# A group's scores and weights traced ahead of the previous group's outputs in the mLSTM heads of a hybrid diffusion step

## The chip, the cores and the metric

The kernel runs on one core of one Trainium2 chip. The metric is device time in microseconds (us) of one execution. The engines are called as the profile calls them: PE (TensorE: matmuls and transposes), DVE (VectorE), ACT (ScalarE), POOL (GpSimd), and SP, which issues most of the DMAs.

## The reference, cut to what matters

One layer of a backbone is applied to 1024 latent tokens and 256 context tokens, 1280 tokens in all, 1024 wide. The layer has three branches: centred pooling, spatial gating, and a bidirectional mLSTM with 4 heads of 128. The change lies in the mLSTM branch, which for a chunk of tokens computes

```python
m_t = jnp.maximum(inter, jnp.max(dmat, axis=2))
w_intra = jnp.exp(dmat - m_t[:, :, None, :])
w_inter = jnp.exp(inter - m_t)
s = jnp.einsum('bthd,bshd->btsh', qc, kc) * w_intra
num = jnp.einsum('btsh,bshd->bthd', s, vc) + w_inter[..., None] * jnp.einsum('bthd,bhde->bthe', qc, C)
den = jnp.sum(s, axis=2) + w_inter * jnp.einsum('bthd,bhd->bth', qc, n)
h = num / jnp.maximum(jnp.abs(den), jnp.exp(-m_t))[..., None]
```

once forward and once backward; the two `h` are added, normalised over each head and later gated. The other branches, the output projection and a feed-forward part follow.

## The kernel before, in words

Tokens are handled in ten chunks of 128, which form three groups (`GROUPS`): chunks 0 to 3, 4 to 7, and the context chunks 8 and 9. Dense projections use weights split in a high and a low part, three matmuls per product (`dense`, L117). `u`, the layer's normalised input, fills 40 of the 59 row buffers of the pool `sp` (`slot`, 128x512 each). A head's k, q and v fill 8 of them (`evict_kqv`, L343), `vn`, the rows of the gating branch, ten (L684).

`head` (L574) works on one head in this order.

- L575 to L591: transposes of k and v (tiles `tk`, `tv`), copied into parts of `z`, the row buffer of 128 x 10240 words that earlier held the input rows.
- L601 to L612: the scan over the chunks' states, matmuls `kv` and a DVE update each (L606), which leaves all states `S` in `z`.
- L615 to L667, a loop over the three groups, in two steps that the change pulls apart. The first (L619 to L641) makes scores and weights: scores `st` on PE (L622), row maxima spread over partitions `rb` (L626), then for each direction `w` = exp(rb + column terms + mask) times scores (L630, L632, L633) and `e` = exp(rb + state maximum) times q (L638, L640). The second (L642 to L667) makes the outputs: for each chunk `pv`, the product of `w` with v plus that of `e` with the state (L649, L651), the denominators (L654 to L656), both directions' sum in `hn` (L657, L658), squares (L659); then for the group the reciprocal root of the mean square (L129 on DVE, L130 on POOL), the scaling (L663), the transposes `th` (L664), the eviction `yc` (L666) and its DMA (L667).

The PSUM tiles `st`, `rb`, `pv`, `th`, `tk`, `tv`, `kv` share five buffers (`ps_sd`, L78); the dense products and `sv` share three others (`ps_mm`, L75). `w`, `e`, `yc` share five SBUF buffers (`tmp`, L72).

What is traced behind a head: the projections of the next one (`head_proj`, L565, L674), and behind the last head the gating branch's `sv` (L679 to L694): two column halves q of ten row tiles, 24 matmuls of 256 columns each, evicted by ACT into `vn[i]` (L693), for which half 0 takes row buffers. Its weights come in two parts per half; the low part is made by POOL (L94 with `eng=G`). Then come the pooling projections `xp` (L842 on) and the windows, which use `z` again.

The order on the engines is not that of the text. The framework plans it (`schedule_with_timeline_sim=True`, L1545): on each engine an instruction earlier in the text goes first among those that the plan holds to be ready, and later text fills what is left. From L276 to L431 the order is pinned by hand (`Pinned`, L35); the heads are not.

Of the kernel before, what the change touches and what calls it, by code (L numbers as in the profile page):

```python
# [14 lines left out]
P = 128  # L15
# [5 lines left out]
GROUPS = ((0, 512), (512, 512), (1024, 256))  # L21
# [27 lines left out]
def hybrid_step(  # L49
# [13 lines left out]
    pa, pw = ExitStack(), ExitStack()  # L63
# [5 lines left out]
    def slot(name, dt=F32R):  # L69
        return sp.tile([P, 512], dt, tag="s", name=name)  # L70

    def tmp(name, dt=F32):  # L72
        return tp.tile([P, 512], dt, tag="t", name=name)
# [4 lines left out]
    def ps_sd(name):  # L78
        return pp.tile([P, 512], F32, tag="sd", name=name, bufs=5)

    def small(shape, name, bufs=4):
        return cp.tile(shape, F32, tag=f"sm{shape[-1]}", name=name, bufs=bufs)
# [44 lines left out]
    def rstd_of(ssq, n, name):  # L127
        r = small([P, 16], f"rs_{name}")
        V.tensor_scalar(r[:, :n], ssq, 1.0 / n_of[name[0]], EPS, ALU.mult, ALU.add)  # L129
        G.tensor_tensor(r[:, :n], r[:, :n], neghalf[:, :n], ALU.pow)  # L130
        return r
# [8 lines left out]
    z = cp.tile([P, 10 * D], F32, name="z")  # L140
# [255 lines left out]
    for at, (g, k) in enumerate(steps):  # L396
# [3 lines left out]
        if (g, k) == (1, 2):  # L400
# [4 lines left out]
            for i in range(2):  # L405
                w = slot(f"wgs{i}").rearrange("p (k c) -> p k c", c=P)
# [28 lines left out]
    def chunks(ap):  # L435
        return ap.rearrange("p (c t) -> p c t", t=P)
# [80 lines left out]
    for g in range(3):  # L517
        t0, n = GROUPS[g]
# [34 lines left out]
    vaug = z[:, 1280:2570].rearrange("p (c t) -> p c t", t=129)  # L553
    vs = z[:, 2570:5150].rearrange("p (c d t) -> p c d t", d=2, t=129)
    S = z[:, 5150:7730].rearrange("p (c d t) -> p c d t", d=2, t=129)
    hn2 = [z[:, 9010 + i * 512 : 9522 + i * 512].rearrange("p (c t) -> p c t", t=P) for i in range(2)]

    def proj(idx, name, evict, eng=V, w=None, groups=range(3)):
# [6 lines left out]
    def head_proj(h):  # L565
        tiles = {}
        kq = kq0 if h == 0 else slot(f"kq{h}", F32)
        for nm, idx in (("k", I_K), ("v", I_V), ("q", I_Q)):
            w, lst = begun.pop(f"{nm}{h}", (None, []))
            tiles[nm] = lst  # L570
            proj(idx + h, f"{nm}{h}", lambda g, ps: lst.append(evict_kqv(nm, h, g, ps, kq)), w=w, groups=range(len(lst), 3))
        return tiles["k"], tiles["v"], tiles["q"]

    def head(h, kT, vT, qT):  # L574
        for g in range(3):  # L575
            t0, n = GROUPS[g]
            c0, ncn = t0 // P, n // P
            ps = ps_sd(f"tk{h}_{g}")
            for c in range(ncn):
                PE.transpose(ps[:, c * P : (c + 1) * P], kT[g][:, c * P : (c + 1) * P], ident)  # L580
            A.copy(knat[:, c0 : c0 + ncn, :], chunks(ps[:, :n]))
            ps = ps_sd(f"tv{h}_{g}")
            for c in range(ncn):
                PE.transpose(ps[:, c * P : (c + 1) * P], vT[g][:, c * P : (c + 1) * P], ident)
            A.copy(vaug[:, c0 : c0 + ncn, 0:P], chunks(ps[:, :n]))  # L585
            for d in range(2):
                e = EWS[:, c0 : c0 + ncn, d * 4 + h].unsqueeze(2).to_broadcast([P, ncn, P])
                V.tensor_tensor(vs[:, c0 : c0 + ncn, d, 0:P], chunks(ps[:, :n]), e, ALU.mult)  # L588
        V.memset(vaug[:, :, P : P + 1], 1.0)
        for d in range(2):  # L590
            V.tensor_copy(vs[:, :, d, P : P + 1], EWS[:, :, d * 4 + h : d * 4 + h + 1])  # L591

        def kv(c, d):
            ps = ps_sd(f"kv{h}_{c}_{d}")
            PE.matmul(ps[:, 0:129], knat[:, c, :], vs[:, c, d, :], start=True, stop=True)  # L595
            return ps[:, 0:129]

        def dc(c, d):
            return decb[:, d * 4 + h, c : c + 1]

        SP.dma_start(S[:, 0, 0, :], state[h, :, 0, :])  # L601
        SP.dma_start(S[:, 7, 1, :], state[h, :, 1, :])
        for i in range(7):
            for d in range(2):
                c, nx = (i, i + 1) if d == 0 else (7 - i, 6 - i)
                V.scalar_tensor_tensor(S[:, nx, d, :], S[:, c, d, :], dc(c, d), kv(c, d), ALU.mult, ALU.add)  # L606
        fin = tmp(f"fin{h}")[:, 0:258].rearrange("p (d t) -> p d t", d=2)
        for d in range(2):
            c, nx = (8, 9) if d == 0 else (9, 8)
            A.copy(S[:, nx, d, :], kv(c, d))  # L610
            V.scalar_tensor_tensor(fin[:, d, :], S[:, nx, d, :], dc(nx, d), kv(nx, d), ALU.mult, ALU.add)
        A.dma_start(st_out[h], fin)  # L612

        ssq = small([P, 16], f"ssq{h}")
        for g in range(3):  # L615
            t0, n = GROUPS[g]
            c0, ncn = t0 // P, n // P
            hn = hn2[(3 * h + g) % 2]
            st = ps_sd(f"st{h}_{g}")  # L619
            for c in range(ncn):  # L620
                s = slice(c * P, (c + 1) * P)
                PE.matmul(st[:, s], kT[g][:, s], qT[g][:, s], start=True, stop=True)  # L622
            pw, qw = [], []
            for d in range(2):
                rb = ps_sd(f"rb{h}_{g}_{d}")
                PE.matmul(rb[:, :n], selr[:, d * 4 + h : d * 4 + h + 1].to_broadcast([100, P]), rhl[g][0:100, :n], start=True, stop=True)  # L626
                w = tmp(f"w{h}_{g}_{d}")
                for c in range(ncn):
                    s = slice(c * P, (c + 1) * P)
                    V.scalar_tensor_tensor(  # L630
                        w[:, s], rb[:, s], GC[:, c0 + c, d * 4 + h : d * 4 + h + 1], masks[d], ALU.add, ALU.add)
                A.activation(w[:, :n], w[:, :n], AF.Exp)  # L632
                V.tensor_tensor(w[:, :n], w[:, :n], st[:, :n], ALU.mult)  # L633
                pw.append(w)
                e = tmp(f"e{h}_{g}_{d}")
                for c in range(ncn):
                    s = slice(c * P, (c + 1) * P)
                    A.activation(  # L638
                        e[:, s], rb[:, s], AF.Exp, bias=mpb[:, d * 4 + h, c0 + c : c0 + c + 1], scale=1.0)
                V.tensor_tensor(e[:, :n], e[:, :n], qT[g][:, :n], ALU.mult)  # L640
                qw.append(e)  # L641
            for cl in range(ncn):  # L642
                c = c0 + cl
                s = slice(cl * P, (cl + 1) * P)
                pv = ps_sd(f"pv{h}_{c}")
                pvv = pv[:, 0:258].rearrange("p (d t) -> p d t", t=129)
                for d in range(2):
                    inter = not (c == 8 and d == 0) and not (c == 9 and d == 1)
                    PE.matmul(pvv[:, d, :], pw[d][:, s], vaug[:, c, :], start=True, stop=not inter)  # L649
                    if inter:  # L650
                        PE.matmul(pvv[:, d, :], qw[d][:, s], S[:, c, d, :], start=False, stop=True)  # L651
                den = small([P, 2, 1], f"den{h}_{c}")
                em = EM[:, c, :].rearrange("p (d h) -> p d h", d=2)[:, :, h]
                A.activation(den[:, :, 0], pvv[:, :, P], AF.Abs)  # L654
                V.tensor_tensor(den[:, :, 0], den[:, :, 0], em, ALU.max)  # L655
                V.reciprocal(den, den)  # L656
                A.activation(hn[:, cl, :], pvv[:, 0, 0:P], AF.Copy, scale=den[:, 0, :])  # L657
                V.scalar_tensor_tensor(hn[:, cl, :], pvv[:, 1, 0:P], den[:, 1, :], hn[:, cl, :], ALU.mult, ALU.add)  # L658
                A.activation(vs[:, c, 0, 0:P], hn[:, cl, :], AF.Square, accum_out=ssq[:, c : c + 1])  # L659
            r = rstd_of(ssq[:, c0 : c0 + ncn], ncn, f"h{h}_{g}")  # L660
            ps = ps_sd(f"th{h}_{g}")
            for cl in range(ncn):
                A.activation(hn[:, cl, :], hn[:, cl, :], AF.Copy, scale=r[:, cl : cl + 1])  # L663
                PE.transpose(ps[:, cl * P : (cl + 1) * P], hn[:, cl, :], ident)  # L664
            yc = tmp(f"yc{h}_{g}")
            A.activation(yc[:, :n], ps[:, :n], AF.Copy, scale=ccol[:, C_GM + h : C_GM + h + 1])  # L666
            SP.dma_start(scr_yc[h, :, t0 : t0 + n], yc[:, :n])  # L667

    qkv = head_proj(0)
    for h in range(H):  # L670
        cur = qkv
        head(h, *cur)
        if h + 1 < H:
            qkv = head_proj(h + 1)  # L674
# [4 lines left out]
    for q in range(2):  # L679
        wq = [load_w(w_sv[q, hf], f"sv{q}_{hf}", eng=G) for hf in range(2)]  # L680
        for i in range(NT):
            g, o = (i * P) // 512, (i * P) % 512
# [356 lines left out]
    for ri, r in enumerate(ORDER):  # L1039
        scr = (scr_ya, scr_yb, scr_yc)[r]  # L1040
        ys = [[] for _ in range(4)]
        for g in range(3):
            for kc in range(4):
                t0, n = GROUPS[g]
# [10 lines left out]
        for d in range(KT):  # L1055
            if d % 2 == 0:
                wb = [load_half(w_branch[r, d // 2][:, i * 512 : i * 512 + 512], f"wb{r}_{d}_{i}") for i in range(2)]
            for g in range(3):
                t0, n = GROUPS[g]
# [494 lines left out]
```

## Time and profile before

| | us |
|---|---|
| three timed runs | 1955.17, 1954.14, 1947.21 |
| their median | 1954.14 |
| the profiled execution's own time | 1949.2 |
| its span, first to last instruction | 1947.4 |
| PE busy | 1910.0 |
| DVE busy | 1301.5 |
| ACT busy | 848.8 |
| POOL busy | 380.8 |
| the four heads, first `tk` to last `th` | 141.5 to 417.1 |

The timed runs lie within 8 us of each other. The profiled execution lies between the lowest of them and the median, 4.9 us below the median. "Busy" is the time in which an engine had at least one instruction of its kind under way; the granted clock beside it says how fast PE ran in that time. A wait is idle time of an engine, put down to the instruction that released it.

### The profile page before, as it was taken

Reading aid. Unit: us, or ns where it says so; the run is one execution under the profiler, and the core shown is the slowest. Engines: PE = TensorE matmul, PEld = TensorE weight load, DVE = VectorE, ACT = ScalarE, POOL = GpSimd, SP = SyncE. Lnnn points to the kernel's source line nnn. Section 1 sums busy time; section 2 is a strip of 40 time slices with the busy share of each in tenths; the row PEclk is TensorE's granted clock in tenths of the full one; section 3 lists DMA queues with packets and bytes.
Section 4 is the critical chain, followed back from the end, with each engine's and each line's share of the span. In section 5 each row is a group of like instructions: output and inputs, shape, how many; then the busy total and the mean of one; then the engine's idle time right before and its main releaser. Section 6 shows DMA issues by size and latency. Waiting matters only on the chain.

```text
span 1947.4 us, 28196 instructions
## 1 busy us (share of the span) xinstructions
PE 1910.0 (98%) x10142; PEld 1632.4 (84%) x10142; DVE 1301.5 (67%) x2234; ACT 848.8 (44%) x1771; POOL 380.8 (20%) x381
## 2 busy tenths in 40 slices
PE   9999998999999999999999999999999999999998
PEld 5878887988888888888888888888888888888886
DVE  6574345469597878776675589887766655654665
ACT  6443365542433333342113375555455545443443
POOL 1100011064022422220000015444431210000003
PEclk9999998999999999999999999999999999999999
DMA  9120111115443444459522435776774596655544
GB/s 371 74 73 33 42 42 39 34 57 186 139 165 129 157 141 153 146 198 363 187 93 98 152 119 213 252 270 243 260 260 140 188 333 202 207 176 151 161 137 161
DMA packets 152774, 318.56 MB, mean 164 GB/s; under 512 B 17934, under 2 KB 42226, under 8 KB 150586
## 3 DMA queue, kind: packets, MB, share of 16 engines
q1 hardware_dynamic: 109082, 223.35, 34.7%
q0 software_dynamic: 15520, 57.75, 7.9%
q10 hardware_dynamic: 28032, 35.67, 5.1%
q8 instruction: 79, 1.29, 0.3%
q14 instruction: 61, 0.50, 0.1%
HBM read 220.21 MB, written 95.98 MB: 162 GB/s over the span
## 4 chain that ended last, share of the span: by engine, by line
PE 65%; DMA 8%; POOL 4%; DVE 4%; issue 2%; ACT 1%; SPq 0%; POOLq 0%; ACTq 0%; DVEq 0%
PE w L1421 6%; PE w L1422 6%; PE w L1423 6%; DMA z<-in_w_ff 4%; POOL z L1260 3%; PE pb L1068 3%; PE pb L1069 3%; PE pb L1070 3%; DMA scr_t<-z 3%; PE fT_g L904 2%; PE fT_g L902 2%; PE fT_g L903 2%; PE po L1188 2%; PE po L1186 2%; PE po L1187 2%; PE fB_g L902 2%
## 5 line engine op out<-in xcount | busy, mean ns | idle before, releaser
L1260 POOL TENSOR_TENSOR z<-z 128x512 f32<-128x512 f32 x64 | 99.9, 1561 | 121.6 <-DMA z<-in_w_ff 118.9
L547 POOL PARTITION_ALL_REDUCE acc<-acc x16 | 54.4, 3437 | 224.5 <-DVE acc L541 148.1
L959 DVE TENSOR_TENSOR z<-z 128x512 f32<-128x512 f32 x120 | 95.3, 794 | 2.7
L541 DVE SCALAR_TENSOR_TENSOR acc<-z,scond,acc 128x512 f32<-128x512 f32 x112 | 82.2, 780 | 0.0
L1375 POOL TENSOR_TENSOR rs_y<-rs_y,neghalf 128x1 f32<-128x1 f32 x10 | 9.9, 989 | 332.5 <-DVE rs_y L1374 332.4
L1226 ACT ACTIVATE z<-z 128x512 f32<-128x512 f32 x64 | 40.5, 632 | 71.4 <-DVE z L968 38.8
L985 ACT ACTIVATE z<-z 128x512 f32<-128x512 f32 x56 | 35.3, 632 | 64.0 <-DVE z L968 18.6
L630 DVE SCALAR_TENSOR_TENSOR w<-rb,gcol,cst 128x128 f32<-128x128 f32 x80 | 21.8, 344 | 35.5 <-PE rb L626 35.5
L1074 DVE TENSOR_TENSOR sg<-pb,sg 128x512 f32<-128x512 f32 (+1 forms) x48 | 28.7, 600 | 24.3 <-PE pb L1070 24.2
L130 POOL TENSOR_TENSOR rs_h<-rs_h,neghalf 128x4 f32<-128x4 f32 (+1 forms) x12 | 11.8, 983 | 150.8 <-DVE rs_h L129 150.5
L1227 ACT ACTIVATE z<-z 128x512 f32<-128x512 f32 x64 | 40.3, 629 | 1.1
L750 POOL TENSOR_TENSOR z<-z 128x256 f32<-128x256 f32 (+13 forms) x20 | 37.6, 1888 | 12.7 <-ACT z L735 6.2
L893 ACT CAST hi_wb<-raw_wb 128x512 fp32r<-128x512 f32 x24 | 14.8, 620 | 56.4 <-PE pb L1069 45.7
L1189 DVE TENSOR_TENSOR po<-po,gt 128x512 f32<-128x512 f32 (+1 forms) x24 | 14.6, 607 | 35.5 <-PE po L1188 35.4
L1251 POOL DMA_DIRECT2D scr_s<-x x48 | 26.2, 547 | 54.8 <-DVE x L1245 49.1
L548 POOL TENSOR_TENSOR acc<-acc,bt 1x512 f32<-1x512 f32 x16 | 22.8, 1440 | 61.0 <-issue 61.0
L1192 ACT ACTIVATE po<-z 128x512 f32<-128x512 f32 (+1 forms) x24 | 12.7, 530 | 48.4 <-DVE z L1191 34.1
L606 DVE SCALAR_TENSOR_TENSOR z<-z,dmb,kv 128x129 f32<-128x129 f32 x56 | 17.0, 346 | 23.1 <-PE kv L595 23.0
L1075 DVE TENSOR_TENSOR z<-z,sg 128x512 f32<-128x512 f32 (+1 forms) x48 | 28.6, 600 | 1.1
L649 PE MATMUL pv<-z,w 128*128 128x129 f32 x160 | 25.9, 283 | 3.3 <-DVE w L633 3.3
L655 DVE TENSOR_TENSOR den<-den,gcol 128x2 f32<-128x2 f32 x40 | 6.8, 178 | 29.9 <-ACT den L654 29.2
L588 DVE TENSOR_TENSOR z<-tv,gcol 128x512 f32<-128x512 f32 (+1 forms) x24 | 14.4, 602 | 18.2 <-ACT z L585 17.9
(5350 smaller groups left out, 7248.7 us busy)
## 6 DMA issues: line engine op xcount, KB each, us to landing
z<-in_w_ff SPq DMA_DIRECT2D x64, 512.0 KB, 5.8
z<-in_w_ada SPq DMA_DIRECT2D x64, 256.0 KB, 3.1
scr_t<-z POOLq DMA_DIRECT2D x16, 1024.0 KB, 4.5
z<-in_w_in SPq DMA_DIRECT2D x28, 512.0 KB, 4.4
scr_g<-z ACTq DMA_DIRECT2D x48, 256.0 KB, 2.0
sg<-scr_g SPq DMA_DIRECT2D x48, 256.0 KB, 4.6
scr_h<-z ACTq DMA_DIRECT2D x48, 256.0 KB, 3.7
scr_s<-x POOLq DMA_DIRECT2D x48, 256.0 KB, 4.7
```

Of the source, the lines that this page charges most:

```text
L541: V.scalar_tensor_tensor(acc[j], raw, scond[:, k, j : j + 1], acc[j], ALU.mult, ALU.add)
L547: G.partition_all_reduce(acc[j], acc[j], P, bass.bass_isa.ReduceOp.add)
L902: PE.matmul(ps, whi[:, s], ahi, start=first and k == ks[0], stop=False)
L959: V.tensor_tensor(out, x, y, op)
L1068: PE.matmul(pb[:, :n], whi[:, s], yh, start=kc == 0, stop=False)
L1069: PE.matmul(pb[:, :n], whi[:, s], yl, start=False, stop=False)
L1070: PE.matmul(pb[:, :n], wlo[:, s], yh, start=False, stop=kc == 3)
L1226: A.activation(t, t, AF.Relu)
L1260: G.tensor_tensor(out, x, y, ALU.subtract)
L1421: PE.matmul(banks[j], h_[:, s], rh, start=fp == 0, stop=False)
L1422: PE.matmul(banks[j], l_[:, s], rh, start=False, stop=False)
L1423: PE.matmul(banks[j], h_[:, s], rl, start=False, stop=fp == NFP - 1)
```

## The change

The first step of a group becomes a function `weighted(g)` that returns the `w` and `e` tiles, the second a function `outputs(g, pw, qw)`. They are called in the order weighted(0), weighted(1), outputs(0), weighted(2), outputs(1), outputs(2). No instruction is added or removed, and no shape changes. Two groups' weights are alive at a time, so some of them move out of the five `tmp` buffers: the `w` tiles of group 1 go to two new views of `z` (columns 7730 to 8753), and the `e` tile of the backward direction of each group goes to the columns of `z` that the same group's `hn` takes afterwards. That leaves three `tmp` buffers for groups 0 and 2, one for group 1, and one for each `yc`.

```diff
+    wz = [z[:, 7730 + i * 512 : 8242 + i * 512] for i in range(2)]
+    hnz = [z[:, 9010 + i * 512 : 9522 + i * 512] for i in range(2)]
     hn2 = [z[:, 9010 + i * 512 : 9522 + i * 512].rearrange("p (c t) -> p c t", t=P) for i in range(2)]
...
         ssq = small([P, 16], f"ssq{h}")
-        for g in range(3):
+
+        def weighted(g):
             t0, n = GROUPS[g]
             c0, ncn = t0 // P, n // P
-            hn = hn2[(3 * h + g) % 2]
             st = ps_sd(f"st{h}_{g}")
...
-                w = tmp(f"w{h}_{g}_{d}")
+                w = wz[d] if g == 1 else tmp(f"w{h}_{g}_{d}")
...
-                e = tmp(f"e{h}_{g}_{d}")
+                e = hnz[(3 * h + g) % 2] if d == 1 else tmp(f"e{h}_{g}")
...
                 qw.append(e)
+            return pw, qw
+
+        def outputs(g, pw, qw):
+            t0, n = GROUPS[g]
+            c0, ncn = t0 // P, n // P
+            hn = hn2[(3 * h + g) % 2]
             for cl in range(ncn):
...
             SP.dma_start(scr_yc[h, :, t0 : t0 + n], yc[:, :n])
+
+        ahead = weighted(0)
+        for g in range(3):
+            following = weighted(1) if g == 0 else weighted(2) if g == 1 else None
+            outputs(g, *ahead)
+            ahead = following
```

## The prediction

> **What bounds the kernel now.** I read the page first, then the busy time by stretch over the heads, then PE's waits there, then the timelines around those waits.
>
> ```profile
> span 1947.4 us, 28196 instructions
> PE 1910.0 (98%) x10142; PEld 1632.4 (84%) x10142; DVE 1301.5 (67%) x2234; ACT 848.8 (44%) x1771; POOL 380.8 (20%) x381
> ...
> PEclk9999998999999999999999999999999999999999
> ```
>
> PE works for 1910.0 of 1947.4 us, so an edit that adds and removes no matmul can win at most the 37.4 us in which PE stands still, and what a lowered clock costs. The clock row has one slice below 9, the seventh (292 to 341 us), which lies in the third head. The page cannot say whose idle time the 37.4 us is, so I cut the heads at the first transpose `th` of each group.
>
> In the next rows the columns are the stretch, its length, then busy time and instructions of PE, PEld, DVE, ACT and POOL, the granted clock, the DMA share and GB/s.
>
> ```profile
> 164.00:184.80 20.80, 20.80 (x125) 18.40 (x124) 8.66 (x28) 9.93 (x35) 1.04 (x1) 1.00 0.12 36
> ...
> 261.80:276.40 14.60, 14.24 (x120) 13.80 (x119) 7.54 (x25) 10.11 (x35) 3.37 (x2) 1.00 0.18 60
> 276.40:284.70 8.30, 6.14 (x49) 5.51 (x47) 3.94 (x15) 4.92 (x19) 0.69 (x1) 1.00 0.08 32
> 284.70:300.20 15.50, 15.32 (x130) 15.08 (x131) 8.23 (x23) 5.55 (x19) 0.00 (x0) 1.00 0.03 10
> 300.20:313.10 12.90, 11.14 (x93) 10.51 (x92) 7.55 (x28) 8.33 (x35) 1.01 (x1) 1.00 0.06 17
> 313.10:329.20 16.10, 11.56 (x94) 10.98 (x94) 9.51 (x26) 11.29 (x40) 4.26 (x2) 0.95 0.13 46
> 329.20:339.90 10.70, 9.01 (x47) 8.44 (x47) 3.94 (x15) 6.02 (x23) 0.70 (x1) 0.60 0.23 86
> ...
> 357.40:375.70 18.30, 18.30 (x156) 18.21 (x155) 7.36 (x26) 11.08 (x46) 1.36 (x3) 1.00 0.02 9
> ```
>
> Length less PE's busy time, from 261.8 to 339.9: 0.36 + 2.16 + 0.18 + 1.76 + 4.54 + 1.69 = 10.7 us. That is the end of the second head and the whole third. In the first head (164 to 184.8) and the fourth (357.4 to 375.7) PE is never idle, though the same chain of steps runs there: later text fills it. So PE bounds the heads except where filler is short.
>
> What the 10.7 us wait for:
>
> ```profile
> PE th L664 <- ACT z L663: 6.3, 3, 4.5
> ...
> PE pv L649 <- DVE w L633: 3.3, 2, 1.6
> ```
>
> Before `th`, the transposes of the scaled outputs, 6.3 us in three waits; before `pv`, for the weights of the same group, 3.3 us in two. The remaining 1.1 us are small.
>
> And the clock:
>
> ```profile
> 328.00:332.00 4.00, 2.40 (x10) 2.00 (x10) 1.13 (x4) 1.60 (x5) 0.75 (x1) 0.50 0.71 254
> 332.00:336.00 4.00, 2.74 (x13) 2.77 (x14) 1.60 (x4) 2.76 (x10) 0.00 (x0) 0.50 0.17 66
> 336.00:340.00 4.00, 3.98 (x26) 3.78 (x26) 1.21 (x7) 2.17 (x11) 0.70 (x1) 0.77 0.00 0
> ```
>
> At clock 0.50 half of PE's busy time is lost: 2.40/2 + 2.74/2 + 3.98 x 0.23 = 1.2 + 1.4 + 0.9 = 3.5 us. It follows the longest wait. So the heads hold 10.7 + 3.5 = 14.2 us that a better order could win. The other 26.7 us of idle time lie outside 261.8 to 339.9 and have nothing to do with the loop.
>
> **Why filler is short, and what the change does to it.** The third head in PE's order:
>
> ```profile
> 307.77 1.06 PE L651 MATMUL pv<-z,e 128*128 128x129 f32 x8
> ...
> 313.07 0.33 PE L664 MATMUL th<-cst,z 128*128 128x128 f32 x1 [1.37 <-ACT z L663]
> 313.24 1.06 PE L622 MATMUL st<-qT,kT 128*128 128x128 f32 x8
> ...
> 318.11 0.83 PE L649 MATMUL pv<-z,w 128*128 128x129 f32 x6
> ...
> 324.43 0.28 PE L692 MATMUL sv<-lo_sv,u7c 128*128 128x256 f32 x1
> 329.24 0.47 PE L664 MATMUL th<-cst,z 128*128 128x128 f32 x1 [4.53 <-ACT z L663]
> ...
> 333.26 1.20 PE L649 MATMUL pv<-z,w 128*128 128x129 f32 x4 [1.63 <-DVE w L633]
> ...
> 335.83 0.56 PE L690 MATMUL sv<-hi_sv,u0h 128*128 128x256 f32 x1
> ```
>
> Two things are to be seen. First, `st` of the next group follows the first `th` of the group ahead at once (313.07, 313.24), and it does so in all eight places of the trace, though k and q have long been there. These are the first and the last:
>
> ```profile
> 174.71 0.39 PE L651 MATMUL pv<-z,e 128*128 128x129 f32 x2
> ...
> 184.78 0.49 PE L664 MATMUL th<-cst,z 128*128 128x128 f32 x3
> 185.10 0.39 PE L622 MATMUL st<-qT,kT 128*128 128x128 f32 x2
> ...
> 398.88 0.27 PE L664 MATMUL th<-cst,z 128*128 128x128 f32 x1
> 398.99 0.39 PE L622 MATMUL st<-kq 128*128 128x128 f32 x2
> ```
>
> The five PSUM buffers that `th` and `st` share seem to be handed out in the order of the text. So the plan cannot pull scores forward by itself; the text must. (The first head has 9.7 us of other work between the end of `pv` and `th`; the third has 4.3.) Second, no `sv` matmul runs between 324.43 and 335.83. The reason is in ACT's evictions of `sv`:
>
> ```profile
> 301.30 0.37 ACT L693 COPY vn<-sv 128x256 f32<-128x256 f32 x1 [0.85 <-PE st L622]
> ...
> 306.66 0.37 ACT L693 COPY vn<-sv 128x256 f32<-128x256 f32 x1 [0.76 <-DVE e L640]
> ...
> 314.33 0.37 ACT L693 COPY vn<-sv 128x256 f32<-128x256 f32 x1 [0.44 <-PE st L622]
> ...
> 319.70 0.37 ACT L693 COPY vn<-sv 128x256 f32<-128x256 f32 x1 [0.76 <-DVE e L640]
> ...
> 334.49 0.37 ACT L693 COPY vn<-sv 128x256 f32<-128x256 f32 x1 [0.49 <-DVE e L640]
> ```
>
> Each waits for a head's `st` or `e`, the last readers of k and q, because `vn` takes the row buffers that they free. Three `sv` tiles fill the three PSUM buffers, and a fourth needs an eviction. So the weights step doles out the filler, one tile per half step, and after 319.70 the next comes at 334.49.
>
> *Removed, the waits before `pv`.* Weights are ready a step before their `pv`: the 2 x 1.63 = 3.3 us go. Their cover is then the previous group's output chain, which from the end of `pv` (307.77 + 1.06 = 308.8) to `th` (313.07) takes 4.3 us at its shortest here.
>
> *Moved, the weights on DVE and ACT.* DVE sets their pace:
>
> ```profile
> L630 DVE SCALAR_TENSOR_TENSOR w<-rb,gcol,cst 128x128 f32<-128x128 f32 x60 | 16.3, 344 | 33.5 <-PE rb L626 33.5
> L640 DVE TENSOR_TENSOR e<-e,qT 128x512 f32<-128x512 f32 x12 | 8.3, 692 | 2.2 <-ACT e L638 1.6
> L633 DVE TENSOR_TENSOR w<-w,st 128x512 f32<-128x512 f32 x12 | 8.1, 679 | 0.3 <-ACT w L632 0.3
> ```
>
> A 512-column group takes 8 x 16.3/60 + 2 x 8.3/12 + 2 x 8.1/12 = 2.2 + 1.4 + 1.35 = 4.9 us of DVE, the context group half, 2.5. These now stand in DVE's order ahead of the denominators of the group before, and ACT's exponentials likewise. Queued behind them are den, `hn`, the squares, POOL's root and at the end `th` on PE. Bound of the delay: 0, if they fit into DVE's waits for ACT and PE, to 4.9 + 2.5 = 7.4 us a head; I take 3.7, the middle, since DVE is busy for only 7.55 of 12.9 us in the stretch from 300.2.
> What a head saves in return: `pv` of group 1 follows `th` of group 0 directly instead of 318.11 - 313.07 = 5.0 us later, `pv` of group 2 that of group 1 instead of 333.26 - 329.24 = 4.0 us later. Net per head 9.0 - 3.7 = 5.3 us, between 1.6 and 9.0.
>
> *What that is worth.* Not 5.3 us a head: where PE was full, the shorter chain only leaves filler for later. But that is what the third head lacks. Three heads shorter by 5.3 us each need 16 us less filler up to the third head's end (4.8 to 27); the hole is 10.7 us of idle time. And k and q of group 1 are freed with those of group 0, those of the context before outputs(1), so the evictions now at 314.33 to 334.49 come a step earlier. With filler the `th` waits should go as in the first and the fourth head, and with the 4.53 us wait the clock loss.
>
> *Residue.* When half 0 of `sv` ends, half 1 needs its weights:
>
> ```profile
> 324.39 2.34 POOL L94 TENSOR_TENSOR lo_sv<-raw_sv,hi_sv 128x1024 fp32r<-128x1024 f32 x1 [11.80 <-ACT hi_sv L93]
> ...
> 326.84 1.91 POOL L130 TENSOR_TENSOR rs_h<-rs_h,neghalf 128x4 f32<-128x4 f32 x1
> ```
>
> The last low part is done at 326.73, 2.0 us after `sv` ended at 324.71, and the head's root stood behind it on POOL. That seam stays, wherever it falls; I keep 2.2 us of idle time for it and the small waits, between 0 and 4.5.
>
> *At no cost:* no instruction is added; the new views of `z` are read by the `pv` matmuls that `hn` waits for already; the DMAs of `yc` move with outputs, past nothing else on SP.
>
> The sum: 10.7 + 3.5 - 2.2 = 12.0 us. Against the profiled execution's 1949.2 that is 1937.2; against the median of 1954.1 it is 1942.1. I forecast **1940 us**, between the two. About 0.5% (9.8 us) is what a measurement of this kernel can tell from no change.
>
> The row on the clock speaks of a cost of 3.5 us for one wait of 4.53 us, and of none for the waits of 1.37 and 1.63 us. The Trainium skill (TensorE: Matmul & The Clock Gate, "What's actually happening") has the clock halved after an idle window of some 3.4 us and restored after as much busy time; by it, an estimate, the wait would cost 3.4/2 = 1.7 us and the sum be 10.2. The trace has more, half clock from 328 to nearly 338, and by the trace's 3.5 I go.
>
> **The rivals.**
>
> *The hole only moves.* The seam of `sv` or the slots still run out inside a head, since ten `sv` tiles need ten freed buffers either way. Then the 3.3 us before `pv` go, and of the 6.3 before `th` and the 3.5 of clock about a third to a half: a gain of 3.3 + 3.3 = 6.6 to 3.3 + 4.9 = 8.2, some 1942 us by the profiled run, 1947 by the median. For it: the seam falls where the head ends now. Against: the 16 us of filler left over.
>
> *The plan was not held by the text.* If `st` ran late for another reason than buffer order, the order stays much as it is, with a gain of 0 to 3: 1946 to 1954. Against it stand the eight places.
>
> *Slower: weights bar the outputs.* Five PSUM buffers less three that `st` and two `rb` of group 1 hold leave two for the four `pv` of group 0, and den sits behind 4.9 us of weights on DVE. It decides if filler is short there: then PE waits 4.9 us longer before `th` of group 0 and 2.5 before that of group 1 in the third head, 2.5 in the second, and a second long wait halves the clock again: -3.3 + 4.9 + 2.5 + 2.5 + 3.5 = +10.1, 1959 us by the profiled run. Against it: the first head's filler, 9.7 us between `pv` and `th`, would cover it there, and k and q are freed earlier.
> The Trainium skill (same page, "Architectural detail: the array is 16× 32×32, not 1× 128×128") has ACT and DVE strictly in order, which speaks against this change as this rival does; the timelines here show no instruction overtaking, and cannot show what the new order costs.
>
> **How the numbers follow.** Forecast case (gain 10 to 14) 0.52; the hole moves 0.28; no effect 0.10; slower 0.10. Faster by over 0.5% takes the first, 0.52; within 0.5% the two middle ones, 0.38; slower 0.10. The range: all 14.2 us won from the lowest run, 1947.2 - 14.2 = 1933; at the top no gain from the median, with the runs' scatter of a microsecond, 1955. The slower case and half of the no-effect case lie outside.
>
> **What would show it.** Right: `st` and `rb` of group 1 before the first `pv` of group 0; no wait of PE for DVE L633; PE idle time in the heads under 4 us; no clock below 0.9 in the heads; evictions L693 of the third head in pairs. Wrong: waits of PE for L663 of 6 us or more, a clock slice of 8 that has only moved, or DVE L655 starting over 4 us later after `pv` than now with PE idle meanwhile. If the total falls by over 15 us, something outside the heads moved, which I have not foreseen.

## The result and the profile after

The kernel with the change takes 1941.72 us (median of 5 runs, 1940.36 to 1941.95), the kernel before 1954.14 us (5 runs beside them, 1947.21 to 1956.44). The ratio is 0.9944, 95% interval 0.9922 to 0.9967: 0.56% faster (0.33% to 0.78%). The forecast was 1940 us. The profiled execution takes 1940.9 us, 8.3 less than that of before.

The page of the kernel after, the rows that answer to the three of before:

```profile
span 1939.1 us, 28222 instructions
PE 1904.2 (98%) x10142; PEld 1628.1 (84%) x10142; DVE 1306.1 (67%) x2234; ACT 848.7 (44%) x1771; POOL 376.6 (19%) x381
...
PEclk9999999999999999999999999999999999999999
```

The slice below 9 has gone from the clock row. PE's idle time is 34.9 us, against 37.4. The code behind the heads has moved down by 17 lines; in the heads, `st` is now L626, `pv` L659 and L661, the scaling L673, `th` L674, `sv` L707, its evictions L710 and L711.

The same execution by stretch (columns as before: length, then busy time of PE, PEld, DVE, ACT and POOL, clock, DMA share, GB/s), the heads in the first two rows, the stage behind them in the others:

```profile
240.00:300.00 60.00, 59.67 (x436) 56.05 (x435) 25.70 (x84) 30.53 (x104) 7.45 (x5) 1.00 0.11 38
300.00:360.00 60.00, 55.98 (x464) 54.57 (x463) 29.66 (x94) 35.11 (x132) 5.44 (x6) 1.00 0.11 37
400.00:480.00 80.00, 78.39 (x429) 66.39 (x428) 72.61 (x76) 26.27 (x49) 47.00 (x41) 1.00 0.42 141
480.00:520.00 40.00, 39.58 (x210) 33.55 (x209) 19.89 (x33) 16.06 (x28) 0.00 (x0) 1.00 0.43 147
```

The heads hold 0.33 + 4.02 = 4.4 us of idle time; before it was 10.7. Behind them, where the kernel before was idle for 0.9 us, there are now 1.61 + 0.42 = 2.0. PE's waits in the heads after:

```profile
PE sv L707 <- ACT sv L711: 2.2, 4, 0.8
PE th L674 <- ACT z L673: 1.3, 1, 1.3
PE pv L659 <- ACT yc L676: 0.8, 1, 0.8
```

The waits for the weights are gone, those for the scaling are down from 6.3 to 1.3. Here is PE in the third head, the order first:

```profile
299.34 1.06 PE L626 MATMUL st<-qT,kT 128*128 128x128 f32 x8
...
300.70 1.05 PE L626 MATMUL st<-qT,kT 128*128 128x128 f32 x8
...
307.81 0.38 PE L659 MATMUL pv<-z,w 128*128 128x129 f32 x2
...
318.61 0.33 PE L674 MATMUL th<-cst,z 128*128 128x128 f32 x1 [1.32 <-ACT z L673]
...
331.76 0.27 PE L674 MATMUL th<-cst,z 128*128 128x128 f32 x1
...
340.03 0.27 PE L674 MATMUL th<-cst,z 128*128 128x128 f32 x1
```

`st` of group 1 (300.70) now stands ahead of the first `pv` of group 0 (307.81). ACT's evictions of `sv` in the middle of the same head, and the step of DVE that frees the last row buffers of q ahead of the second of them:

```profile
310.75 0.37 ACT L710 COPY vn<-sv 128x256 f32<-128x256 f32 x1
323.98 0.37 ACT L710 COPY vn<-sv 128x256 f32<-128x256 f32 x1
327.96 0.37 ACT L710 COPY vn<-sv 128x256 f32<-128x256 f32 x1 [0.78 <-PE sv L709]
```

```profile
323.51 0.43 DVE L644 TENSOR_TENSOR z<-z,kq 128x256 f32<-128x256 f32 x1
```

There is still a long gap between evictions, 13 us (before: 15), but it ends at 323.98 instead of 334.49, right behind the step in which the weights of the context group, made early, read q for the last time; in the kernel before, the same step released the eviction that ends the gap. That eviction is the tenth and last of half 0. Half 1 of `sv` writes into the same rows and needs no new buffers; its evictions wait only for `sv` itself. Its first matmul stands at

```profile
324.79 0.39 PE L707 MATMUL sv<-hi_sv,u0h 128*128 128x256 f32 x1 [0.22 <-ACT sv L711]
```

and before at 335.83. In the head, from its first `st` to its last `th`, eight `sv` tiles begin; before there were five. (`sv` is the filler here: matmuls of a later stage that PE takes when the heads have none ready.) So far the steps of the prediction are to be seen. The length of the heads did not go as forecast. From the first `st` to the last `th` of each it was 56.9, 44.3, 41.5 and 59.5 us before, and is 49.5, 47.4, 41.0 and 53.8 after: the second became longer, and the third is about as long as it was.

For what follows one more measure is needed, since the start of the program, with the same instructions in every kernel here, takes 163.0 to 166.6 us. I take the *stretch* from the first `st` to the last `p_su` matmul on `u6l`, a fixed instruction near the end of the gating branch. Its two ends, before and then after, each from a tile's list (count, duration, first and last start):

```profile
L622 PE MATMUL st<-qT,kT x16: 270/275/275, 164.0 to 186.0; 128*128 128x128 f32 x16
...
L124 PE MATMUL p_su<-u6l,hi_su x8: 389/389/389, 433.3 to 509.9; 128*128 128x512 f32 x8
```

```profile
L626 PE MATMUL st<-qT,kT x16: 270/275/275, 166.6 to 170.8; 128*128 128x128 f32 x16
...
L124 PE MATMUL p_su<-u6l,hi_su x8: 389/389/395, 425.1 to 503.2; 128*128 128x512 f32 x8
```

345.9 us became 336.6, 9.3 less; the start of this execution was 2.6 longer, and what follows the stretch 1.6 shorter, together the 8.3. What follows the stretch takes between 1434.3 and 1441.0 us in the fourteen profiles of this document, without a pattern that goes with the edits. So a difference of a few microseconds between two totals need not come from the heads, and the stretch is the better measure.

### The profile page after: what moved, and what is told of

Same layout as the page of the kernel before. It is cut to its first block, busy times and chain, and to the rows that moved or that the text cites. A ratio compares the mean times of both kernels' runs of the same rounds, so it can differ in the third digit from the quotient of the medians.

```text
span 1939.1 us, 28222 instructions
## 1 busy us (share of the span) xinstructions
PE 1904.2 (98%) x10142; PEld 1628.1 (84%) x10142; DVE 1306.1 (67%) x2234; ACT 848.7 (44%) x1771; POOL 376.6 (19%) x381
## 4 chain that ended last, share of the span: by engine, by line
PE 86%; DVE 5%; DMA 4%; ACT 2%; POOL 2%; issue 1%; SPq 0%; POOLq 0%; ACTq 0%; DVEq 0%
PE w L1438 6%; PE w L1439 6%; PE w L1440 6%; PE pb L1086 3%; PE pb L1085 3%; PE pb L1087 3%; PE fT_g L921 3%; PE fT_g L919 3%; PE fT_g L920 3%; PE fT L919 3%; PE fT L920 3%; PE fT L921 3%; PE fB L921 2%; PE fB L920 2%; PE fB L919 2%; PE fB_g L921 2%
## 5 line engine op out<-in xcount | busy, mean ns | idle before, releaser
L1206 DVE TENSOR_TENSOR po<-po,gt 128x512 f32<-128x512 f32 (+1 forms) x24 | 14.6, 609 | 35.4 <-PE po L1205 35.3
L634 DVE SCALAR_TENSOR_TENSOR w<-rb,gcol,cst 128x128 f32<-128x128 f32 x48 | 13.3, 343 | 24.5 <-PE rb L630 24.5
L590 DVE TENSOR_TENSOR z<-tv,gcol 128x512 f32<-128x512 f32 (+1 forms) x24 | 14.2, 601 | 17.5 <-ACT z L587 17.3
```

## The experiments

All times below are medians of at least 5 runs beside runs of the kernel before on the same chip, whose median was 1952 to 1954 us. The table is worked out from each profile: the last `th` and the end of the stretch, both counted from the first `st`; PE's idle time from 240 to 360 us ("heads": the second and the third) and behind the heads (400 to 520); the clock from 300 to 360. Each kernel has one profile.

| kernel | last `th` | stretch | idle, heads | clock | idle, behind | us | ratio to before (95%) |
|---|---|---|---|---|---|---|---|
| before | 252.9 | 345.9 | 10.7 | 0.91 | 0.9 | 1954.14 | 1 |
| before_again | 252.9 | 345.2 | 10.7 | 0.91 | 0.4 | 1951.64 | 1.0000 (0.9991 to 1.0009) |
| room_only | 250.1 | 344.8 | 10.4 | 0.91 | 0.4 | 1952.1 | 0.9998 (0.9988 to 1.0007) |
| order_only | 267.2 | 358.1 | 15.4 | 0.94 | 3.4 | 1961.77 | 1.0051 (1.0038 to 1.0064) |
| hold | 243.1 | 343.6 | 7.5 | 0.91 | 1.4 | 1945.24 | 0.9965 (0.9951 to 0.9978) |
| third_only | 253.1 | 346.8 | 6.4 | 1.00 | 7.4 | 1949.55 | 0.9988 (0.9979 to 0.9996) |
| fourth_only | 241.6 | 344.5 | 10.4 | 0.91 | 0.4 | 1951.34 | 0.9997 (0.9987 to 1.0007) |
| third_fourth | 247.3 | 338.6 | 6.4 | 1.00 | 1.4 | 1942.15 | 0.9951 (0.9937 to 0.9965) |
| all_but_third | 238.8 | 341.7 | 8.4 | 0.91 | 0.4 | 1944.05 | 0.9959 (0.9947 to 0.9972) |
| after | 244.6 | 336.6 | 4.4 | 1.00 | 2.0 | 1941.72 | 0.9944 (0.9922 to 0.9967) |
| before_vnact | 252.9 | 345.2 | 10.7 | 0.91 | 0.4 | 1953.24 | 1.0008 (1.0000 to 1.0017) |
| third_vnact | 253.1 | 341.8 | 6.4 | 1.00 | 4.5 | 1945.39 | 0.9965 (0.9953 to 0.9978) |
| after_vnact | 244.5 | 335.2 | 4.4 | 1.00 | 0.9 | 1940.2 | 0.9938 (0.9925 to 0.9950) |
| after_both | 244.6 | 335.3 | 4.4 | 1.00 | 1.1 | 1938.67 | 0.9921 (0.9905 to 0.9938) |

**room_only and order_only: the two halves of the change alone.** room_only has the buffers of the change and the old order, order_only the new order with all weights in the five `tmp` buffers.

```diff
-        ahead = weighted(0)
         for g in range(3):
...
+            outputs(g, *weighted(g))
```

```diff
-                w = wz[d] if g == 1 else tmp(f"w{h}_{g}_{d}")
+                w = tmp(f"w{h}_{g}_{d}")
...
-                e = hnz[(3 * h + g) % 2] if d == 1 else tmp(f"e{h}_{g}")
+                e = tmp(f"e{h}_{g}_{d}")
```

> The new places for w and e, but weighted(g) directly followed by outputs(g), the old order. Both theories: st still follows th, so nothing changes against the kernel before, 1947 to 1956 us, 10 to 11 us of PE idle time in the heads and the lowered clock in the third.

> The changed order, but w and e all in the five buffers of tmp as before: scores of the next group go to PE early, its weights must wait for room until the outputs of the group ahead have been read. Filler theory: st of group 1 is early and frees k, so half of the evictions come early, q is freed late: third head idle for 5 to 7 us, 1943 to 1947 us. Weights theory: the waits before pv come back with the late weights, 1948 to 1952 us.

The room alone does nothing that can be measured; the order without room is 0.5% slower, 15 us above the upper end of its filler range and 10 above that of the other: neither theory had foreseen it. PE's waits from 240 to 360 us of order_only:

```profile
PE sv L707 <- ACT sv L711: 7.4, 3, 4.0
PE th L674 <- ACT z L673: 3.4, 1, 3.4
PE pv L659 <- DVE z L668: 2.5, 3, 1.9
```

With five buffers for two groups' weights the heads get longer (the last `th` 14 us later than before), and PE stalls for 15.4 us in them; the clock is lowered in the second head too (0.91 from 240 to 300 us). The room wins no time of its own; it is what the order needs.

**hold: the new order, but k and q freed late.** The kernel after, in which one-column reads on DVE keep the row buffers of k and q taken until about when the kernel before gave them up (four small reads a head are added, into an unused column; the expectation counts five).

```diff
+                if cl == 0 and g > 0:
+                    V.tensor_tensor(pad1[:, 1:2], qT[g][:, 0:1], hn[:, 0, 0:1], ALU.add)
...
+                if cl == 0 and g < 2:
+                    V.tensor_tensor(pad1[:, 0:1], kT[g + 1][:, 0:1], hn[:, 0, 0:1], ALU.add)
```

> The changed kernel, with k of the next group read once more (one column, on DVE) after the scaling of the outputs ahead of it, and q of a group once more after its first output: the row buffers of k and q come free about when they did in the kernel before, while scores and weights are still made a group earlier. Five one-column DVE instructions a head are added. If the gain comes from filler (vn's evictions take the buffers that k and q leave), the waits before pv stay away, 3.3 us, but those before th come back in the third head with 4 us or more and perhaps the lowered clock: 1945 to 1950 us. If it comes from the weights being ready and the chain being shorter, freed buffers don't matter: 1941 to 1943 us.

Its longest waits of PE in the heads, the eviction that ends the gap in the third head, and the first matmul of half 1:

```profile
PE th L676 <- ACT z L675: 6.3, 2, 4.5
```

```profile
333.07 0.37 ACT L714 COPY vn<-sv 128x256 f32<-128x256 f32 x1
```

```profile
333.88 0.58 PE L711 MATMUL sv<-hi_sv,u0h 128*128 128x256 f32 x1 [0.68 <-ACT sv L715]
```

Half 1 starts 9 us later than in the change, and with that the long waits before `th` are back, 6.3 us as before, and the lowered clock. The heads are as short as in the change (49.5, 47.6, 41.2 and 52.7 us). Nor are its `th` late: the first ones of the third head's first two groups start at 313.26 and 330.00, with the change at 318.61 and 331.76. PE waits for them because it has nothing else to do. So these waits hang on when k and q come free, not on the length of the heads. The stretch is 7.0 us longer than with the change, 2.3 shorter than before. The medians show less of it: 1945.24 us is 0.35% faster than before, so by them more than half of the gain is left.

**third_only, fourth_only, third_fourth, all_but_third: the order head by head.** Buffers as in the change; the new order only for some of the heads.

```diff
+        if h == 2:
             ahead = weighted(0)
...
+        else:
+            for g in range(3):
+                outputs(g, *weighted(g))
```

The others have `h == 3`, `h >= 2` and `h != 2`.

> The new order in the third head alone, the old one in the other three. If what counts is that the third head's own k and q are freed earlier, most of the gain is here: 1942 to 1945 us, third head idle under 5 us. If it needs the filler that shorter first and second heads leave over, as the prediction's sum had it, less than half: 1947 to 1951 us.

> The new order in the fourth head alone; buffers as in the change. Theory of two bounds from the first score to the last p_su matmul: PE's own work with its stalls (345.9 us in the kernel before, of which 14 are the stalls and the lowered clock of the second and third head), and the chain of the four heads plus the DVE work behind them (252.9 us to the last transpose, 93 more behind it). Before, both are equally long. The fourth head alone shortens only the chain, by 6 to 8 us; PE's stalls stay: 1949 to 1953 us, 0 to 2 us less than before, the stretch 344 to 346 us. With the third head's order alone the gain was 0.1%, with both 11 us. Rival: the fourth head's order is what wins, and the third head's nothing: 1942 to 1945 us.

> The new order in the third and the fourth head, the old one in the first two; buffers as in the change. With the new order in the third head alone the kernel took 1949.6 us: the third head lost its stalls (idle time 300 to 360 us from 8.0 to 4.0, clock full), but 7.4 us of new idle time came between 400 and 520 us. Theory: that time is won only if the work behind the heads, which hangs on DVE (scaling of vn, window sums), starts earlier too, and it starts when the last head and the last sv tile are done. With the fourth head shorter by about 4.6 us as in the change, the new idle time falls to 2 to 3 us: 1942 to 1945 us. Rival one: the first two heads must be shorter too, since their filler is what is left over behind the third; then the fourth head's new order changes little: 1948 to 1951 us. Rival two: the fourth head, short of filler now, stalls itself (idle time over 2 us between 360 and 420): 1946 to 1949 us.

> The new order in the first, second and fourth head, the old one in the third. Theory: the third head's waits depend on its own order and on when its own row buffers come free, not on filler saved by the first two; its 8 us of idle time and the lowered clock (3.5 us) stay, and the gain is what the waits of the second head and the earlier fourth head give, 3 to 6 us: 1946 to 1949 us. Rival, the working of the prediction: two heads shorter by 5.3 us each leave 10.6 us of filler for the third, whose waits before the transposes go though its order is the old one: idle time 300 to 360 us under 4 us, clock full, 1941 to 1944 us.

In third_only the third head is as in the change: half 1 starts at 325.31, the long waits and the lowered clock are gone. Yet the stretch is no shorter. Its PE waits behind the heads, and its busy time there by stretch:

```profile
PE mx L844 <- ACT ya L798: 4.1, 1, 4.1
PE mx L844 <- DVE vn L720: 2.8, 2, 1.6
```

```profile
416.00:422.00 6.00, 6.00 (x40) 5.48 (x39) 6.00 (x3) 2.79 (x5) 5.84 (x3) 1.00 0.32 109
422.00:430.00 8.00, 5.15 (x32) 4.40 (x31) 8.00 (x9) 2.19 (x3) 5.73 (x6) 1.00 0.00 0
430.00:440.00 10.00, 10.00 (x57) 8.72 (x56) 9.96 (x8) 2.19 (x3) 1.04 (x1) 1.00 0.21 80
```

DVE (the third busy column) has 6.00 of 6, 8.00 of 8 and 9.96 of 10 us, and PE stands still for 2.85 us in the second row: filler that was used up in the third head seems to be missing here, and PE waits for the scaled `vn`. (The longer wait, 4.1 us, ends later, at 484.24.) That DVE work was on the path before the change too. The chain of waits of the kernel before, behind the heads:

```profile
413.81 2.69 DVE lo_xp L94
416.50 9.38 DVE vn L699 x10
```

The scaling needs a root from POOL, which stands there behind that of the last head:

```profile
410.57 0.71 POOL L130 TENSOR_TENSOR rs_h<-rs_h,neghalf 128x2 f32<-128x2 f32 x1
411.25 1.95 POOL L130 TENSOR_TENSOR rs_v<-rs_v,neghalf 128x10 f32<-128x10 f32 x1
```

So here it begins only behind the outputs of the last head (in the kernel before `lo_xp` comes in between); in before, third_only, third_fourth and after it begins between 0.5 and 3.8 us ahead of the last `th`. So the stretch has two lower bounds. One is PE: its own work is about 345.9 - 11.1 - 3.5 = 331.3 us (the stretch of before less its idle time and the lost clock; the same working gives 329.7 to 332.3 in the other kernels), plus its stalls and what the clock loses. The other is the chain: the heads up to the last `th`, and about 92 us behind it (93.0, 93.7, 91.3 and 92.0 in before, third_only, third_fourth and after; 102.9 in fourth_only, where the chain has time to spare). For the kernel before, 331.3 + 14.6 and 252.9 + 93.0 are one length divided in two ways, and show nothing by themselves; that both bounds stand there, the edits of one bound alone have to show.
fourth_only shortens the chain by 11.3 us and leaves the stalls: 331.3 + 10.4 + 0.4 + 3.5 = 345.6, measured 344.5, and no change of the time. third_only removes stalls and leaves the chain: 253.1 + 93 = 346, measured 346.8, and 0.12%. third_fourth does both: 331.3 + 6.4 + 1.4 = 339.1, measured 338.6, and 0.49%, where the change itself has 0.56%. (The PE sums use each run's own idle time; they show that nothing else costs PE time, not how much it would idle.) Alone the two heads gave 0.12% and 0.03%, together 0.49%.
all_but_third asks whether the first two heads save filler for the third. They do not. Its PE waits in the heads:

```profile
PE th L674 <- ACT z L673: 6.0, 2, 4.6
PE pv L659 <- DVE w L637: 1.6, 1, 1.6
```

The third head's waits before `th` are as they were (6.0 against 6.3), and so is the clock, though the heads in front of it are in the new order. The expectation's time was missed: the two heads, the earlier chain and 2.3 us less idle time made 1944 us, where 1946 to 1949 was expected. The stretch fell by 4.2 us to 341.7 (the sum for PE gives 331.3 + 8.4 + 0.4 + 3.5 = 343.6, 2 us too much), the median by more: 0.41%, of the change's 0.56%, and the two intervals overlap. Against fourth_only the stretch is 2.8 us shorter and the median 7.3 us lower; where the rest of that comes from no profile shows. So how the medians' gain divides among the heads stays open; the account by heads rests on the stretch, where this kernel has 4.2 of the 9.3 us.

**vnact: the chain behind the heads shortened by itself.** The ten scalings of `vn` go from DVE to ACT, in the kernel before, in third_only and in the change.

```diff
-        V.tensor_scalar(vn[i], vn[i], r[:, i : i + 1], None, ALU.mult)
+        A.activation(vn[i], vn[i], AF.Copy, scale=r[:, i : i + 1])
```

> The kernel before, with the ten scalings of vn behind the heads on ACT instead of DVE (9.5 us of DVE). Theory of two bounds: the chain behind the heads gets 5 us shorter, as it did with the third head's order (343.5 against 347.0 us... of whole span 1943.5 against 1947.0), but PE's stalls in the heads stay, so the gain is at most the 0.9 us of idle time that the kernel before has between 400 and 520 us: 1950 to 1953 us. Rival: the chain behind the heads alone sets the time: 1946 to 1949 us.

> The new order in the third head alone, as in the run of 1949.6 us, and the ten scalings of vn behind the heads on ACT instead of DVE, where they took 13.9 us of a stretch in which DVE is never idle. Theory that DVE's block behind the heads takes the third head's gain back: the waits of PE for the scaled vn and for ya (idle time of 7.4 us between 400 and 520 us, and about 1.5 us of lowered clock) go: 1941 to 1945 us. Rival: PE idles there because the filler is used up, whoever scales vn; the waits then stand before other instructions: 1947 to 1951 us.

> The change as it is, with the ten scalings of vn on ACT instead of DVE. In the change PE is idle for only 2.0 us between 400 and 520 us, so by the theory that DVE's block behind the heads costs PE time only where filler is short, the gain is at most that: 1939 to 1942 us (0 to 2 us faster than the change). Rival: DVE's block also sets when the later stages begin; 11 us less of it moves them up and lets over 3 us be won: under 1938 us. If ACT's own work behind the heads (copies into the window buffers) is held up by 10 scalings of 0.6 to 1.2 us: 1943 to 1946 us.

The two bounds once more: in the kernel before, where the stalls still bound it, a shorter chain gives nothing (1.0008). In third_only the same edit cuts the stretch by 5.0 us, with the last `th` where it was (behind it 88.7 us instead of 93.7). In the change, which has 2.0 us of idle time left there, it cuts 1.4. The medians of before_vnact and third_vnact lie 0.2 and 0.4 us above their expected ranges.

**before_again: the kernel before once more.**

> The kernel before, unchanged, to see how far its executions differ from one to the next: its timed runs lie between 1947 and 1956 us, those of the change within 2 us. Theory: a ratio of 1 within 0.2%, and a profile whose heads are as in the first profile; where its total differs by several microseconds, the difference lies outside 240 to 520 us (idle time of 1120 to 1240 us, the start). Rival: the stalls in the heads themselves differ from run to run, by over 2 us, so that the change also wins by making the heads steady.

The heads repeat: the same lengths within 0.1 us, 10.7 us of idle time. The timed runs of the kernel before differ by 9 us (1947.95 to 1956.62), and the profiled execution was the lowest of twelve. So of the 12.4 us between the medians some 4 are not in the profiles, which differ by 8.3. Where the longer runs lose them no profile shows; that stays open.

**after_both: the low part of the `sv` weights on DVE too.** The change with `vn` scaled on ACT and the seam's POOL work taken away.

```diff
-        wq = [load_w(w_sv[q, hf], f"sv{q}_{hf}", eng=G) for hf in range(2)]
+        wq = [load_w(w_sv[q, hf], f"sv{q}_{hf}") for hf in range(2)]
```

> The change, with the ten scalings of vn on ACT as in the run of 1940.2 us, and with the low part of the sv weights made by DVE instead of POOL, so that the heads' roots on POOL cannot stand behind it. Theory: after the change no matmul waits for that low part any more (the sv waits of the third head are for ACT's squares, 2.2 us), so the seam that the prediction kept 2.2 us for is not what is left: 1939 to 1942 us, no difference from the change that can be measured, and the 4.0 us of idle time from 300 to 360 us stay. Rival, the residue of the prediction: the low part on POOL holds the root and the transposes behind it (1.3 us of wait) and the evictions; idle time 300 to 360 us falls to 2 us or less, and with the shorter chain behind the heads the time to 1936 to 1938.5 us. If 4 x 1.2 to 2.2 us more of DVE work bars the weights of the heads: 1942 to 1946 us.

Idle time in the heads is the same 4.4 us, the stretch the same as in after_vnact. So the seam is not what is left. The median is the lowest of all, 1938.67 us, 0.3 below the expected range, but its interval overlaps with that of the change (0.9905 to 0.9938 against 0.9922 to 0.9967), and the stretch does not show where more than 1.3 us would come from.

## Why the prediction was right, and where not

*The forecast* held: 1941.72 for 1940, faster by 0.56%, just over the 0.5% that it named; the interval, 0.33% to 0.78%, has the 0.5% within it. In the profiles the gain is 8.3 us where the sum said 12.0. That the number came so near is in part luck: some 4 of the 12.4 us between the medians are in no profile, and the route to the rest was partly another.

*The pool of 14.2 us in the heads* was read rightly: 10.7 fell to 4.4 and the clock's 3.5 went, 9.8 together. Of these, 1.1 were lost again behind the heads, where the idle time rose from 0.9 to 2.0.

*The buffers handed out in the order of the text.* `st` of group 1 moved with the text (300.70), as said. Whether it was the buffers that had held it, or the plan's preference for earlier text, no run separates.

*The signs.* `st` and `rb` ahead of the first `pv`, no wait for the weights, the full clock: all there. PE's idle time in the heads was to fall under 4 us and is 4.4, and the evictions do not come in pairs.

*The waits before `pv`.* Gone, as said. Beside third_fourth, the new order in the first two heads is worth 338.6 - 336.6 = 2.0 us of the stretch, which is the second head's idle time: 2.40 us from 240 to 300 there, 0.33 in the change.

*The row buffers freed earlier.* This was a half sentence of the prediction ("so the evictions now at 314.33 to 334.49 come a step earlier"), and it is why the waits before `th` went: hold, which takes only this back, brings back 6.3 us of them and the lowered clock.

*The step that failed* is "Net per head 9.0 - 3.7 = 5.3 us", and with it "Three heads shorter by 5.3 us each need 16 us less filler". The first three heads changed by -7.4, +3.1 and -0.4 us, under 5 us together. In the third head the way from the first `st` to the first `th` grew from 12.9 to 318.61 - 299.34 = 19.3 us, 6.4 more instead of 3.7; the two later steps shrank from 16.2 and 10.6 to 13.2 and 8.3, 5.3 less instead of 9.0. One reason seems to stand in the timeline: the fourth `pv` of group 0 comes late.

```profile
310.26 0.39 PE L661 MATMUL pv<-z 128*128 128x129 f32 x2
...
312.51 0.39 PE L659 MATMUL pv<-z,w 128*128 128x129 f32 x2
```

It starts 2.25 us behind the last row of the third, with `st` and two `rb` of group 1 in three of the five PSUM buffers, as the slower rival had said (that this held it up is read from the order, no run tried it); but filler covered it, and none of its waits (4.9, 2.5) came. The filler was not saved by shorter heads; it was let in by freed buffers: three more `sv` tiles within the same length.

*What was left out* is worse than the step that failed. The sum counted each microsecond won on PE in the heads as one of the total. But the prediction read its views only up to 416 us, and the chain behind the heads was about as long as PE's work with its stalls. With the third head's stalls gone and the other heads as they were, the gain was 0.12%. The fourth head, 5.7 us shorter with the change, which the prediction left out of its account, is what let the third head's gain count (third_fourth: 0.49%).

*The residue.* 2.2 us were kept (0 to 4.5) for the seam of `sv`; 4.4 were found, and they are not the seam. The low part of the second half now ends early, at 319.25, ahead of need (324.79):

```profile
315.81 1.01 POOL L130 TENSOR_TENSOR rs_h<-rs_h,neghalf 128x4 f32<-128x4 f32 x1 [34.72 <-PE sv L708]
316.88 2.37 POOL L94 TENSOR_TENSOR lo_sv<-raw_sv,hi_sv 128x1024 fp32r<-128x1024 f32 x1
```

2.2 us are waits of `sv` for ACT's squares, which hold its PSUM tiles. The 1.32 us before `th` come from ACT too: the scaling L673 stands behind two conversions of weights, though its root was done at 316.82.

```profile
315.76 1.05 ACT L93 CAST hi_sv<-raw_sv 128x1024 fp32r<-128x1024 f32 x1 [0.31 <-PE sv L708]
317.20 1.04 ACT L93 CAST hi_xp<-raw_xp 128x1024 fp32r<-128x1024 f32 x1 [0.39 <-PE sv L708]
318.15 1.28 ACT L673 ACTIVATE z<-z,rs_h 128x128 f32<-128x128 f32 x4
```

*The rivals.* "The hole only moves" is nearest to what third_only did: the hole moved, not within the heads but behind them. "Slower" came true in order_only, at 0.5%, where the new order has no room; with the room it did not.

## What to carry to other kernels

Idle time of the busiest engine is worth removing only as far as the chain of the other engines behind it is shorter too: before counting the gain, follow the chain past the stage, to the next place where the engine waits. If two bounds are equally long, an edit of one alone shows little or nothing, and both together show the gain, so an edit that measures as no change is not yet useless. And filler has two limits, how much there is and when its buffers let it in; look at what its evictions wait for before hoping to save any.

## What the runs showed of the hardware

The lowered clock lasted a whole number of periods of 3.41 us: in the fourteen profiles, from the first `st` to 1900 us, each stretch at half clock is 3.41, 6.83 or 10.24 us long. In third_only a wait of 4.13 us ended at 484.24, and PE then worked without a stop. The rows go period by period:

```profile
481.84:485.25 3.41, 1.01 (x7) 0.93 (x7) 3.41 (x7) 1.81 (x3) 0.00 (x0) 1.00 0.65 244
485.25:488.66 3.41, 3.41 (x10) 2.64 (x9) 3.38 (x7) 1.00 (x2) 0.00 (x0) 0.50 0.69 219
488.66:492.08 3.42, 3.42 (x16) 2.82 (x15) 2.73 (x5) 0.00 (x0) 0.00 (x0) 1.00 0.37 141
```

After a period in which PE was idle for 2.40 us the clock was half for one period, in which PE was never idle. In the kernel before, the wait of 4.53 us was followed by 1.76 us of work, another wait of 1.63 us and then work without a stop, and the clock was half for three:

```profile
324.19:327.60 3.41, 0.52 (x5) 0.32 (x3) 2.38 (x2) 1.93 (x8) 3.10 (x2) 1.00 0.00 0
327.60:331.01 3.41, 1.77 (x9) 1.77 (x10) 0.47 (x2) 1.28 (x4) 1.15 (x1) 0.50 0.77 273
331.01:334.43 3.42, 1.79 (x8) 1.42 (x8) 2.52 (x8) 2.33 (x7) 0.00 (x0) 0.50 0.29 111
334.43:337.84 3.41, 3.41 (x18) 3.41 (x17) 1.07 (x7) 1.85 (x9) 0.00 (x0) 0.50 0.00 0
```

The first holds the end of the long wait (1.64 us idle), the second the second wait (1.63), and only behind the third, without idle time, is the clock full. So the likely reading is that the second wait, which in the second head did not lower the clock, here put off its return by a period. By these rows the cost was half of 1.77 + 1.79 + 3.41 us, the 3.5 of the prediction; without the second wait, an estimate from the same rows, half of 1.77 + 3.41 = 2.6. That is part of what set the 3.5 apart from the 1.7 worked out by the Trainium skill (TensorE: Matmul & The Clock Gate, "What's actually happening"). Its rule of some 3.4 us of sustained work to release the clock agrees with both tables; the estimate had left out the second wait, and the part of the first that reached into the lowered clock. No run tried it by itself. A long wait is not needed: in hold a single wait of 1.86 us, ended at 313.26, was followed by half clock from 313.51 to 316.92, while 1.63 us in the second head of the kernel before did not lower it.

DVE's scaling of a `vn` row took from half a microsecond to three (473 to 2903 ns in the kernel before). Whether POOL works at the same time makes the difference. The ten of third_only, in three stretches:

```profile
415.35:422.84 7.49, 7.49 (x47) 6.73 (x46) 7.49 (x3) 3.23 (x6) 7.13 (x5) 1.00 0.26 88
422.84:424.81 1.97, 1.97 (x14) 1.74 (x13) 1.97 (x6) 1.74 (x3) 0.05 (x1) 1.00 0.00 0
424.81:429.30 4.49, 1.64 (x13) 1.29 (x11) 4.49 (x4) 0.00 (x0) 4.33 (x3) 1.00 0.00 0
```

While POOL (the fifth busy column) worked on the window sums, three scalings took 7.49 us; while it all but stood still (0.05 us), five took 1.97; when it worked again, two took 4.4. In the ten profiles with this scaling on DVE, the 25 of the 100 that met no work on POOL took 0.47 to 0.48 us each, and every longer one met some. On ACT, in after_vnact, the mean of ten was 711 ns, ten in 6.2 us where DVE had taken 9.5 to 14.6, with POOL at work there too. The Trainium skill (GPSIMD Engine Reference, "1. Specifications") has POOL's access to SBUF shared with VectorE, with contention for VectorE instructions in certain modes or with two SBUF inputs. Whether this scaling is of that kind no run here shows, and no run took POOL's work away.
